# A decoder layer on one core: a rearranged input stage (meta tokens' statistics on ScalarE, first tiles loaded by halves on two queues, bias products moved ahead, first group's splits moved back)

## Chip, core and metric

The kernel runs on one NeuronCore of a Trainium2 chip. The metric is the device time of one execution in microseconds (us). Engines are called as in the profile: PE (TensorE, matrix products and transposes), PEld (its weight loads), DVE (VectorE), ACT (ScalarE), POOL (GpSimd) and SP (SyncE, which here only issues DMAs). DMAs are issued from SP's queue and from ACT's queue.

## The reference

One layer of a hybrid decoder over 1024 tokens of width 1024, with 16 meta tokens put in front. What touches the change is the beginning:

```
h = concatenate([meta_tokens, x])              # 16 + 1024 rows
h = layer_norm(h, in_ln_g, in_ln_b)            # over 1024 columns, eps 1e-5
z = h @ w_in + b_in                            # split into q | k | v | conformer input | gates
...
bias_of(d) = rel_bias[t5_bucket(d)]            # a table of 32 buckets x 8 heads, spread over distances
```

Behind it come sliding-window attention with sinks and the T5 bias, a gated causal convolution, the merge of both by two gates, a residual with a layer norm, and a convolutional feed-forward block with a second residual and norm.

## The kernel before

All activations stay transposed (channels on partitions, tokens on the free axis). Each float32 product is made of three products of rounded halves: an operand is split into `hi` (rounded, a cast on ACT or DVE) and `lo` (the rest, a subtraction on DVE), and PE forms hi·hi, hi·lo and lo·hi.

**The input stage** (lines 170 to 613) has to bring x and the meta tokens in, normalise them, transpose them on PE and make the first three column tiles of z: tile 0 is k, tile 1 is v, tile 2 is the first quarter of q. Tokens come in eight tiles x0 to x7 of 128 rows; the 16 meta rows are tile -1. They are held twice, on partitions 0 to 31 of `xm`, and the normalised ones are written to partitions 96 to 127. Work goes by three groups: group 0 is the meta rows with x0 and x1 (272 columns), group 1 x2 to x4, group 2 x5 to x7 (384 each).

For each group the steps are: `stat` (two bn_stats over 512 columns and one aggregate, on DVE), `table` (reciprocal root, ACT), `newton` (one Newton step in small DVE operations), `norm` (x·r + m in halves of 512 columns, on DVE or ACT), `turns` (PE transposes, 128 channels `k` at a time, into PSUM banks; there are four such banks, tags s and t), `scaled` (ACT: gain and bias of the layer norm, from PSUM to SBUF, which frees the bank), `parts` (the hi and lo of the result), and the products. Group 0 takes a short cut: its first products (`z_first(..., raw=True)`) are plain float32 products of the unsplit operands, so that no split is waited for; its `parts` are only needed by later tiles of z. The groups 1 and 2 go through `lagged`, in which the three tiles follow one another at two steps' distance.

`warm` are 28 products of a matrix of ones that PE does while nothing is there yet. `whi0` and `wlo0` split the first three weights. `evac` empties the sums: k into `kd`, v into `vT`, q (scaled, split) into `qd`.

**Order.** The tile framework orders each engine's instructions by a simulated timeline: lower ranks go first (`rank`, `tc.cur_priority`), and what is ready goes. For the input stage the order is written out by hand: `in_order` gives three chains, `dv`, `ac` and `pe`, whose instructions keep the order of the source on DVE, ACT and PE. What is issued outside these chains (evacuations, loads) finds its place by rank. `load` issues on SP's queue, `store` on ACT's. A queue issues in order, and a waiting entry holds the ones behind it.

**The bias table.** `tab` holds one-hot rows for 564 distances and the 33 x 8 table. Two products (400 and 164 columns) give `vrow`, which goes to DRAM (`v1d`), is spread over 128 partitions (`vd`) and read with skewed patterns into the attention's bias tiles. Before, these products stand on PE behind the third group's last product.

**After the stage** come `residual` (DVE makes h0 for the residual from the normalised tiles, and SP stores it to `h0d`) and `conv_chunk`, whose first two weights (`wt_c1`) are split early. `z_tile` makes one column tile of z over the token groups `ZG` (400, 384 and 256 columns) in the order of the list.

Of the kernel before, what the change touches and what calls it, by code (L numbers as in the profile page):

```python
# [101 lines left out]
def tile_hybrid_layer(  # L102
# [68 lines left out]
    with rank(0):  # L171
        nc.vector.memset(eps, EPS)
        nc.scalar.activation(small.tile([P, 1], F, name="sq"), eps, AF.Abs_reciprocal_sqrt)
# [31 lines left out]
    with rank(25):  # L205
        load(tab[:33], table_in)
# [14 lines left out]
    nc.vector.memset(ones, 1.0 / CW)  # L221
    qb = const.tile([P, 4], F, name="qb")
# [50 lines left out]
    def weights(shape, fill):  # L273
# [4 lines left out]
        with rank({1: 13, 2: 18, 3: 17, 4: 23}.get(n, RK_SPLIT)):  # L278
            last_fill.append(fill(raw))
# [63 lines left out]
    def q_evac(r):  # L343
        def evac(g, a, b, ps):
# [5 lines left out]
            for hl, (put, x) in enumerate(((store, f32(h)), (load, f32(l)))):  # L350
# [48 lines left out]
    def newton(t):  # L399
# [6 lines left out]
        dv(stt(m_, mv[:, :, 0], -1.0, r_, OP.mult, OP.mult))  # L406
# [7 lines left out]
    def norm(t, j, on_dve):  # L414
# [3 lines left out]
        if j < 0:  # L418
            xns[j], to = xm, xm[96:]
        else:  # L420
            xns[j] = to = sp.tile([P, D], F, name="xn", tag="xn", bufs=4) if j < 4 else OB[:, (j - 4) * D:(j - 3) * D]
        for a in range(0, D, 512):
            if on_dve:
                dv(V.tensor_scalar(to[:, a:a + 512], x_[:, a:a + 512], r_[:n, i:i + 1], m_[:n, i:i + 1], OP.mult, OP.add))
            else:
                ac(nc.scalar.activation(to[:, a:a + 512], x_[:, a:a + 512], AF.Identity, bias=m_[:n, i:i + 1],
# [117 lines left out]
    norm(1, 0, True)  # L544
    norm(1, 1, False)
    turns(0, 0, 1, 2, 3)
    stat(2, 2, 3, 4)
# [7 lines left out]
    z_first(0, (0,), 5, 6, 7, raw=True)  # L555
    table(2)
    newton(2)
    whi0(0)
# [3 lines left out]
    z_first(0, (2,), 0, 1, 2, 3, 4, raw=True)  # L562
# [4 lines left out]
    z_first(0, (2,), 5, 6, 7, raw=True)  # L567
# [31 lines left out]

    tc.cur_priority = RK_RESID + 1000  # L600
    vrow = sp.tile([NH, J_LEN], F, name="vrow")
    for a, b in ((0, 400), (400, J_LEN)):
        ps = pat.tile([P, 512], F, name="ps_v", tag="o" if a == 0 else "t", bufs=1 if a == 0 else 2)
        after(nc.tensor.matmul(ps[:NH, :b - a], tab[:, J_LEN:], tab[:, a:b], start=True, stop=True), pe_done[-1])
        after(nc.vector.tensor_copy(vrow[:, a:b], ps[:NH, :b - a]), first_nm)
    load(v1d, vrow)
# [4 lines left out]
    residual(3, -1, 0, 1, 2, 3)  # L611
# [1130 lines left out]
```

## Time and profile before

| | |
|---|---|
| runs (us) | 1282.33, 1282.07, 1282.24; median 1282.24 |
| the profiled execution | 1282.14 us, span 1280.0 us |
| PE, DVE, ACT, POOL busy | 99%, 84%, 46%, 4% of the span |
| granted PE clock, mean | 0.999 |
| DMA | 212.10 MB, 166 GB/s on average; near 420 GB/s from 9 to 19 us |

The page gives busy shares, the span in 40 slices, the DMA queues, the chain of work that ended last and the costliest groups of instructions. The answers of the trace used below are: the chain of waits in order of time (start, duration, what the end of the kernel waited for), tables of busy time in chosen stretches (PE, PEld, DVE, ACT, POOL, granted clock, DMA share, GB/s), groups of instructions by form (count, busy us, mean ns, idle time before and what ended it), the timeline, and the DMA view (packets, sizes, issues, median us from issue to landing). A line number is that of the code above; L117 and L113 are the helpers `store` and `load`.

### The profile page before, as it was taken

The page shows a single profiled execution, that of the slowest core. Times are in us where ns is not written, and L with a number is a line of the kernel's source. Part 1 is how long each engine was busy: PE and PEld are TensorE (multiplying, and loading weights), DVE is VectorE, ACT ScalarE, POOL GpSimd, SP SyncE. Part 2 cuts the span into 40 slices and gives each one's busy share as a digit, 9 for nine tenths or more (in the row PEclk, how much of TensorE's full clock was granted, in tenths as well). Part 3 has the DMA queues.
Part 4 walks back from the last instruction along what each step waited for, and adds up shares of the span by engine and source line. Part 5 has one row for each costly group of instructions (what it writes and reads, how often), then busy time and mean ns, then how long its engine had stood idle before and what let it go on. Part 6 is the DMA issues. An engine that isn't in the chain of part 4 may idle for free.

```text
span 1280.0 us, 21674 instructions
## 1 busy us (share of the span) xinstructions
PE 1267.9 (99%) x8546; PEld 1192.8 (93%) x8546; DVE 1078.7 (84%) x1830; ACT 585.5 (46%) x1063; POOL 53.8 (4%) x28
## 2 busy tenths in 40 slices
PE   9999999999999999999999999999999999999997
PEld 8999999999999999788999999999999997888886
DVE  7899989999987577548899898988989876987697
ACT  7523245545482233344655555455454453435330
POOL 0000000010112231000000000000000000000000
PEclk9999999999999999999999999999999999999999
DMA  7284633332247354222145545454454566989712
GB/s 274 73 306 108 180 95 100 98 95 88 75 136 232 111 157 116 83 99 77 56 172 190 191 178 198 163 194 149 157 190 171 192 242 238 392 291 349 269 60 83
DMA packets 96152, 212.10 MB, mean 166 GB/s; under 512 B 10787, under 2 KB 35939, under 8 KB 95922
## 3 DMA queue, kind: packets, MB, share of 16 engines
q1 hardware_dynamic: 84282, 199.64, 46.1%
q10 hardware_dynamic: 11768, 11.08, 2.7%
q8 instruction: 67, 1.10, 0.4%
q14 instruction: 35, 0.29, 0.1%
HBM read 150.29 MB, written 62.70 MB: 166 GB/s over the span
## 4 chain that ended last, share of the span: by engine, by line
PE 96%; DVE 2%; DMA 1%; ACT 0%; issue 0%; SPq 0%; DVEq 0%; ACTq 0%
PE px L1463 15%; PE py L1463 10%; PE ps_x L1588 9%; PE ps_z L298 8%; PE ps_z L294 8%; PE ps_z L299 8%; PE ps_z L1588 5%; PE pw L1463 5%; PE pz L1463 5%; PE ps_p L298 2%; PE ps_p L299 2%; PE ps_p L294 2%; PE ps_w L294 2%; PE ps_w L299 2%; PE ps_w L298 2%; PE ps_z L510 2%
## 5 line engine op out<-in xcount | busy, mean ns | idle before, releaser
L662 DVE SCALAR_TENSOR_TENSOR FA<-cin,cols,FA 128x1026 f32<-128x1026 f32 x120 | 155.2, 1305 | 0.2
L294 PE MATMUL ps_z<-RHO,whi 128*128 128x384 f32 (+2 forms) x324 | 105.0, 324 | 0.0
L298 PE MATMUL ps_z<-RHC,whi 128*128 128x384 f32 (+2 forms) x324 | 104.9, 324 | 0.0
L299 PE MATMUL ps_z<-RHC,wlo 128*128 128x384 f32 (+2 forms) x324 | 104.2, 321 | 0.0
L298 PE MATMUL ps_z<-RHO,whi 128*128 128x384 f32 (+2 forms) x324 | 104.1, 321 | 0.0
L294 PE MATMUL ps_z<-RHC,whi 128*128 128x384 f32 (+2 forms) x324 | 103.9, 321 | 0.0
L299 PE MATMUL ps_z<-RHO,wlo 128*128 128x384 f32 (+2 forms) x324 | 103.3, 319 | 0.0
L1285 DVE TENSOR_TENSOR RHO<-wr,RHO 128x512 fp32r<-128x512 f32 x94 | 63.5, 684 | 10.3 <-ACT RHO L1284 10.3
L1284 ACT CAST RHO<-wr 128x512 fp32r<-128x512 f32 x94 | 56.8, 620 | 21.3 <-DVE wr L1302 10.5
L265 ACT CAST whi<-wr 128x1024 fp32r<-128x1024 f32 x37 | 38.9, 1052 | 59.4 <-PE ps_z L298 42.0
L294 PEld LDWEIGHTS ps_z<-RHO,whi 128*128 128x128 f32 x324 | 60.9, 188 | 0.6 <-issue 0.3
L299 PEld LDWEIGHTS ps_z<-RHC,wlo 128*128 128x128 f32 x324 | 61.1, 188 | 0.4
L298 PEld LDWEIGHTS ps_z<-RHC,whi 128*128 128x128 f32 x324 | 60.9, 188 | 0.4
L294 PEld LDWEIGHTS ps_z<-RHC,whi 128*128 128x128 f32 x324 | 60.8, 188 | 0.3
L298 PEld LDWEIGHTS ps_z<-RHO,whi 128*128 128x128 f32 x324 | 60.9, 188 | 0.2
L299 PEld LDWEIGHTS ps_z<-RHO,wlo 128*128 128x128 f32 x324 | 61.0, 188 | 0.1
L1302 DVE TENSOR_TENSOR wr<-wr 128x512 f32<-128x512 f32 x88 | 60.1, 683 | 0.2
L1475 ACT COPY FA<-px 128x514 f32<-128x514 f32 (+2 forms) x23 | 13.1, 571 | 81.6 <-PE px L1463 81.6
L268 POOL TENSOR_TENSOR wlo<-wr,whi 128x1024 fp32r<-128x1024 f32 x17 | 42.0, 2474 | 188.4 <-ACT whi L265 177.1
L669 ACT ACTIVATE FA<-ps_z,cols 128x386 f32<-128x386 f32 (+2 forms) x48 | 26.0, 541 | 51.3 <-PE ps_z L299 46.9
L1285 DVE TENSOR_TENSOR ws<-wr,ws 128x512 fp32r<-128x512 f32 x60 | 40.6, 685 | 6.1 <-ACT ws L1284 6.0
L1463 PE MATMUL px<-OA,RHO 128*128 128x258 f32 x324 | 43.5, 283 | 0.0
(456 smaller groups left out, 3583.5 us busy)
## 6 DMA issues: line engine op xcount, KB each, us to landing
wr<-in_w_up_dram SPq DMA_DIRECT2D x44, 512.0 KB, 4.2
wr<-in_w_z_dram SPq DMA_DIRECT2D x30, 512.0 KB, 6.2
fd<-FA SPq DMA_DIRECT2D x44, 256.0 KB, 2.4
OB<-in_w_down_dram SPq DMA_DIRECT2D x21, 512.0 KB, 4.8
FA<-sd SPq DMA_DIRECT2D x15, 512.0 KB, 8.0
qt<-qd SPq DMA_DIRECT2D x28, 256.0 KB, 3.9
td<-OB SPq DMA_DIRECT2D x12, 512.0 KB, 3.2
sums<-fd SPq DMA_DIRECT2D x12, 512.0 KB
```

Of the source, the lines that this page charges most:

```text
L265: ins = nc.scalar.copy(hi, raw)
L268: return (nc.vector if quick else nc.gpsimd).tensor_tensor(lo, raw, f32(hi), OP.subtract)
L294: ins = nc.tensor.matmul(ps, ah, bh, start=i == 0, stop=False)
L298: nc.tensor.matmul(ps, ah, bl, start=False, stop=False)
L299: last = nc.tensor.matmul(ps, al, bh, start=False, stop=i == n - 1)
L662: nc.vector.scalar_tensor_tensor(acc[c], cin[:, j:j + U], wc, acc[c], OP.mult, OP.add)
L669: nc.scalar.activation(t, ps, AF.Tanh, bias=bcol(14 + i), scale=0.5)
L1284: nc.scalar.copy(hi, src)
L1285: ins = nc.vector.tensor_tensor(lo, src, f32(hi), OP.subtract)
L1302: ins = nc.vector.tensor_tensor(*x)
L1463: ins = nc.tensor.matmul(o, x[:, ks], bmat(sub, q, hl, k), start=first and k + j == 0, stop=k == 3 and j == 2, skip_group_check=not first)
L1588: nc.tensor.matmul(banks[i], l[:, ts], r[:, ws], start=first and a and x + k == 0, stop=z and x == len(ops) - 1 and k == 2, skip_group_che ...
```

## The change

- The 16 meta rows are loaded twice by one DMA with a source that repeats them (stride 0), not by two DMAs.
- x0 is loaded in two halves of 512 columns on ACT's queue, ahead of ACT's first instruction; x1 in two halves on SP's. The ranks of the other loads change: the bias table now before the first weight, the third weight before x3.
- The meta tokens' mean, variance, reciprocal root and Newton step go from DVE to ACT (`meta_norm`): two passes over 1024 columns with accumulators, six one-column operations. Group 0's Newton step on DVE then has three operations, not four; `norm` on DVE takes (x - mean)·r and no longer needs m.
- The first normalisations go in three pieces (256, 256, 512 columns); x1's are now on DVE too. The first transposes are of two values of k, then of two more, not of four at once.
- The warm-up has 21 products, not 28. The two products with the bias table follow it; DVE copies their result between the statistics of x2 and x3, and `v1d` is stored there.
- Tile 2 makes all eight raw products of group 0 before the second group's transposes (before: five before, three behind).
- The split of tile 1's weight moves behind the fourth scaling of group 1; statistics of x6 and x7 move back by one or two channels.
- The third group's transposes and products are interleaved in smaller pieces; the splits of group 0 (`parts(0, ...)`) move behind the whole third group, their `hi` onto ACT.
- The first group's stores of k and of the first q part go on SP's queue.
- The first conv chunk's gate tile takes its token groups in the order 1, 2, 0; `residual` begins with x1.

```diff
     with rank(0):
         nc.vector.memset(eps, EPS)
+        x0 = sp.tile([P, D], F, name="x0", tag="x", bufs=8)
+        for a in range(0, D, 512):
+            store(x0[:, a:a + 512], x[0, :P, a:a + 512])
         nc.scalar.activation(small.tile([P, 1], F, name="sq"), eps, AF.Abs_reciprocal_sqrt)
...
     with rank(5):
-        for i in range(2):
-            load(xm[i * NMETA:(i + 1) * NMETA], meta_tokens)
-    xt = []
+        load(xm[:2 * NMETA], dram(meta_tokens, 0, [[0, 2], [D, NMETA], [1, D]]))
+    xt = [x0]
...
-        load(t, x[0, j * P:(j + 1) * P, :])
+        for a, b in ((0, 512), (512, D)) if j == 1 else ((0, D),):
+            load(t[:, a:b], x[0, j * P:(j + 1) * P, a:b])
         xt.append(t)
 
-    for j in range(NB):
-        with rank((10, 11, 14, 15, 16, 20, 21, 22)[j]):
+    for j in range(1, NB):
+        with rank((0, 10, 20, 24, 26, 30, 32, 34)[j]):
             load_x(j)
...
-    with rank(12):
+    with rank(14):
         load(cols, cols_in)
...
-    with rank(25):
+    with rank(16):
         load(tab[:33], table_in)
...
+    c15, eps_h = (const.tile([P, 1], F, name=n) for n in ("c15", "eps_h"))
+    nc.vector.memset(c15, 1.5)
+    nc.vector.memset(eps_h, -0.5 * EPS)
...
-        with rank({1: 13, 2: 18, 3: 17, 4: 23}.get(n, RK_SPLIT)):
+        with rank({1: 18, 2: 28, 3: 22, 4: 36}.get(n, RK_SPLIT)):
...
-    def z_tile(fill, groups, evac, wt=None):
+    def z_tile(fill, groups, evac, wt=None, order=(0, 1, 2)):
         wt = wt or weights([P, KC, P], fill)
-        for g, (a, b) in enumerate(groups):
-            z_group(wt, g, a, b, evac)
+        for g in order:
+            z_group(wt, g, *groups[g], evac)
...
-        store(kd[:, a:b], t)
+        (load if g == 0 else store)(kd[:, a:b], t)
...
-            for hl, (put, x) in enumerate(((store, f32(h)), (load, f32(l)))):
+            for hl, (put, x) in enumerate(((load if g == 0 and r == 0 else store, f32(h)), (load, f32(l)))):
...
-        dv(stt(m_, mv[:, :, 0], -1.0, r_, OP.mult, OP.mult))
+        if t > 1:
+            dv(stt(m_, mv[:, :, 0], -1.0, r_, OP.mult, OP.mult))
...
+    def meta_norm():
+
+        n = 2 * NMETA
+        norms[0] = [None] + [sp.tile([P, 1], F, name=f"{n_}0") for n_ in "trm"]
+        nm, var, v_ = (sp.tile([P, 1], F, name=n_)[:n] for n_ in ("nm", "varm", "vm"))
+        _, t_, r_, m_ = (x_ if x_ is None else x_[:n] for x_ in norms[0])
+        junk = OB[:n, 3 * D:4 * D]
+        act = lambda *a, **k: ac(nc.scalar.activation(*a, **k))
+        act(junk, xm[:n], AF.Identity, scale=-1.0 / D, accum_out=nm)
+        act(junk, xm[:n], AF.Square, bias=nm, scale=1.0, accum_out=var)
+        act(v_, var, AF.Identity, bias=eps_h[:n], scale=-0.5 / D)
+        act(r_, var, AF.Abs_reciprocal_sqrt, bias=eps[:n], scale=1.0 / D)
+
+        act(t_, r_, AF.Identity, scale=v_)
+        act(t_, t_, AF.Identity, bias=c15[:n], scale=r_)
+        act(r_, t_, AF.Identity, scale=r_)
+        act(m_, nm, AF.Identity, scale=r_)
...
-        for a in range(0, D, 512):
+        for a, b in zip(cuts, cuts[1:]):
             if on_dve:
-                dv(V.tensor_scalar(to[:, a:a + 512], x_[:, a:a + 512], r_[:n, i:i + 1], m_[:n, i:i + 1], OP.mult, OP.add))
+                dv(V.tensor_scalar(to[:, a:b], x_[:, a:b], mv[:n, i, 0:1], r_[:n, i:i + 1], OP.subtract, OP.mult))
...
-                with rank(24):
+                with rank(38):
                     load(gb[i], dram(ln0_in, i * D, [[0, P], [1, D]]))
...
-    warm = pat.tile([P, 512], F, name="ps_w", tag="o")
-    for i in range(28):
+    warm = pat.tile([P, 512], F, name="ps_w", tag="mm", bufs=3)
+    for i in range(21):
         pe(nc.tensor.matmul(warm[:, :P], ones, ones, start=True, stop=True))
-    stat(0, -1)
-    table(0)
+    vrow = sp.tile([NH, J_LEN], F, name="vrow")
+    vps = []
+    for a, b in ((0, 400), (400, J_LEN)):
+        ps = pat.tile([P, 512], F, name="ps_v", tag="mm" if a else "o", bufs=3 if a else 1)
+        pe(nc.tensor.matmul(ps[:NH, :b - a], tab[:, J_LEN:], tab[:, a:b], start=True, stop=True))
+        vps.append((a, b, ps))
     stat(1, 0)
-    newton(0)
-    norm(0, -1, False)
+    meta_norm()
     stat(1, 1)
     table(1)
+    cuts = (0, 256, 512, D)
+    for c in zip(cuts, cuts[1:]):
+        norm(0, -1, False, c)
+    newton(1)
+    for c in zip(cuts, cuts[1:]):
+        norm(1, 0, True, c)
+        norm(1, 1, True, c)
+    turns(0, 0, 1)
+    turns(0, 2, 3)
+    stat(2, 2)
+    for a, b, ps in vps:
+        dv(V.tensor_copy(vrow[:, a:b], ps[:NH, :b - a]))
+    with rank(40):
+        load(v1d, vrow)
+    stat(2, 3)
     scalings()
-    newton(1)
-    norm(1, 0, True)
-    norm(1, 1, False)
-    turns(0, 0, 1, 2, 3)
-    stat(2, 2, 3, 4)
+    stat(2, 4)
...
+    whi0(0)
     table(2)
     newton(2)
-    whi0(0)
...
-    z_first(0, (2,), 0, 1, 2, 3, 4, raw=True)
+    z_first(0, (2,), *range(8), raw=True)
     evac(0, 0)
     wlo0(0)
     whi0(2)
     turns(1, 0, 1, 2, 3)
-    z_first(0, (2,), 5, 6, 7, raw=True)
     z_first(0, (1,), *range(8), raw=True)
...
     for k in range(8):
         scaled(1, k)
+        if k == 3:
+            whi0(1)
         parts(1, k, hi_act=(k,))
-        if k == 1:
-            whi0(1)
+        if k == 3:
             wlo0(1)
-        if k in (3, 6):
-            stat(3, 6 if k == 3 else 7)
+        if k in (5, 7):
+            stat(3, 6 if k == 5 else 7)
...
-    lagged(1, (0, 2, 1), range(8))
+    lagged(1, (0, 2, 1), range(9))
     turns(2, 0, 1, 2, 3)
-    lagged(1, (0, 2, 1), range(8, 10))
-    turns(2, 4, 5, 6, 7)
-    lagged(1, (0, 2, 1), range(10, 12))
+    lagged(1, (0, 2, 1), range(9, 12))
     for k in range(8):
         scaled(2, k)
         parts(2, k, hi_act=(1, 3, 5, 7))
-        if k in (3, 4, 5, 6):
-            parts(0, 2 * k - 6, 2 * k - 5)
-    lagged(2, (0, 2, 1), range(12))
+        if k == 1:
+            turns(2, 4, 5)
+            lagged(2, (0, 2, 1), range(2))
+        elif k > 1:
+            if k == 3:
+                turns(2, 6, 7)
+            lagged(2, (0, 2, 1), (k,))
+    lagged(2, (0, 2, 1), range(8, 12))
+    parts(0, *range(8), hi_act=range(8))
     first_nm = dv_done[-1]
-
-    tc.cur_priority = RK_RESID + 1000
-    vrow = sp.tile([NH, J_LEN], F, name="vrow")
-    for a, b in ((0, 400), (400, J_LEN)):
...
-    load(v1d, vrow)
...
-    residual(3, -1, 0, 1, 2, 3)
+    residual(3, 1, -1, 0, 2, 3)
...
-        z_tile(in_cols(10 + c), ZG, g_evac, wt_c1[0] if c == 1 else None)
+        z_tile(in_cols(10 + c), ZG, g_evac, *((wt_c1[0], (1, 2, 0)) if c == 1 else ()))
```

More of the change, by code (lines that the diff above doesn't have):

```diff
@@ L412, in scalings, with norm @@
         dv(V.tensor_scalar(nsink, sink, -1.0, None, OP.mult))
-    def norm(t, j, on_dve):
+    def meta_norm():
[13 more added lines that the diff above has]
+        act(m_, nm, AF.Identity, scale=r_)
+    def norm(t, j, on_dve, cuts=(0, 512, D)):
         x_, n = src_of(j)
@@ L419, in norm @@
             xns[j], to = xm, xm[96:]
+        elif j in xns:
+            to = xns[j]
         else:
             xns[j] = to = sp.tile([P, D], F, name="xn", tag="xn", bufs=4) if j < 4 else OB[:, (j - 4) * D:(j - 3) * D]
-        for a in range(0, D, 512):
+        for a, b in zip(cuts, cuts[1:]):
             if on_dve:
-                dv(V.tensor_scalar(to[:, a:a + 512], x_[:, a:a + 512], r_[:n, i:i + 1], m_[:n, i:i + 1], OP.mult, OP.add))
+                dv(V.tensor_scalar(to[:, a:b], x_[:, a:b], mv[:n, i, 0:1], r_[:n, i:i + 1], OP.subtract, OP.mult))
             else:
-                ac(nc.scalar.activation(to[:, a:a + 512], x_[:, a:a + 512], AF.Identity, bias=m_[:n, i:i + 1],
+                ac(nc.scalar.activation(to[:, a:b], x_[:, a:b], AF.Identity, bias=m_[:n, i:i + 1],
                                         scale=r_[:n, i:i + 1]))
@@ L594, in tile_hybrid_layer @@
         parts(2, k, hi_act=(1, 3, 5, 7))
-        if k in (3, 4, 5, 6):
-            parts(0, 2 * k - 6, 2 * k - 5)
-    lagged(2, (0, 2, 1), range(12))
-    first_nm = dv_done[-1]
-    tc.cur_priority = RK_RESID + 1000
-    vrow = sp.tile([NH, J_LEN], F, name="vrow")
-    for a, b in ((0, 400), (400, J_LEN)):
-        ps = pat.tile([P, 512], F, name="ps_v", tag="o" if a == 0 else "t", bufs=1 if a == 0 else 2)
-        after(nc.tensor.matmul(ps[:NH, :b - a], tab[:, J_LEN:], tab[:, a:b], start=True, stop=True), pe_done[-1])
-        after(nc.vector.tensor_copy(vrow[:, a:b], ps[:NH, :b - a]), first_nm)
-    load(v1d, vrow)
+        if k == 1:
[7 more added lines that the diff above has]
+    parts(0, *range(8), hi_act=range(8))
+    first_nm = dv_done[-1]
     tc.cur_priority = RK_QKV + 3000
```

## The prediction

> **What bounds the kernel now.** First the page: engine totals, and the shares of the chain that ended last.
>
> ```profile
> span 1280.0 us, 21674 instructions
> PE 1267.9 (99%) x8546; PEld 1192.8 (93%) x8546; DVE 1078.7 (84%) x1830; ACT 585.5 (46%) x1063; POOL 53.8 (4%) x28
> ...
> PE 96%; DVE 2%; DMA 1%; ACT 0%; issue 0%; SPq 0%; DVEq 0%; ACTq 0%
> ```
>
> PE is the bound nearly everywhere, so the change can win only where PE does not yet do work that counts, or where it does work that could lie elsewhere. The chain of waits over the first 70 us (start, us, what) shows where:
>
> ```profile
> 0.74 0.40 SPq L113
> ...
> 1.65 3.97 DMA x<-in_x_dram
> ...
> 5.64 1.30 DVE st L391 x2
> ...
> 7.78 1.46 ACT xm L426 x2
> ...
> 9.32 0.30 ACT r L397
> ...
> 9.64 0.17 DVE t L403
> ...
> 9.84 0.17 DVE t L404
> ...
> 10.43 0.56 DVE xn L424
> ...
> 11.03 1.11 PE ps_h L460 x8
> ...
> 12.16 0.58 ACT FA L466
> ...
> 12.79 0.73 PE ps_z L507 x2
> ...
> 16.21 4.01 PE ps_z L507 x18
> 20.22 1.31 PE ps_h L460 x12
> 21.53 4.97 PE ps_z L507 x22
> ...
> 56.06 1.05 PE ps_v L604 x4
> ```
>
> Until 12.79 the chain runs over the load of x0, statistics, a Newton step (9.64 to 10.43), the first normalised half, nine transposes and one scaling. From 12.79 on it is PE alone: I call this moment P0. A table of busy time by stretches (length, PE busy, instructions, clock, DMA share, GB/s) confirms it and dates the warm-up:
>
> ```profile
> 1.00:7.20 6.20, 6.12 (x28) 1.00 0.79 256
> 7.20:10.30 3.10, 3.10 (x30) 1.00 1.01 407
> ...
> 12.80:56.10 43.30, 43.30 (x253) 1.00 0.39 138
> ```
>
> So the whole question is: how much earlier is P0, what leaves the PE stream behind it, and does the stream stay unbroken. All sums are made against the profiled execution, 1282.14 us (1280.0 of span and 2.1 around it); the median of the runs, 1282.24, lies 0.10 above it.
>
> **Bias products, minus 1.05.** The two products with the table (56.06, 1.05 us) move behind the warm-up. Their cover is idle PE: the warm-up is cut from 56 instructions to 42. The first 28 take until 7.2, the other 14 go at 3.10/28 = 0.11 us, to about 8.75; the bias products then end at 9.8. The first useful transpose must be later than that, or the 1.05 is partly paid again. They also wait for the table's load, and every transpose stands behind them on PE; that load is now ahead of the first weight, behind x1 and the columns on SP, and by the reckoning below (151 KB on the slowest engine, 5.8 us at 26 GB/s, from the 2 us at which the first data move) it is there near 8, before the warm-up ends.
>
> **The meta tokens' load.** Two loads of 16 rows become one, whose source is [2 copies, 16 rows, 1024]. The trace has one store of that form: line 809 writes 16 rows as [2 blocks, 8 heads, 128]. The DMA view in the stretch that holds the first meta load alone, then in the one that holds that store:
>
> ```profile
> DMA packets 35, 0.08 MB, mean 35 GB/s; under 512 B 16, under 2 KB 16, under 8 KB 35
> ```
>
> ```profile
> DMA packets 18, 0.01 MB, mean 4 GB/s; under 512 B 2, under 2 KB 18, under 8 KB 18
> ...
> rd<-rt ACTq DMA_DIRECT2D x1, 8.0 KB
> ```
>
> The meta load of 16 rows has 16 tiny packets beside its data; the store of 16 pieces has two. I read a tiny packet as the end of one DMA engine's share, so the store ran on two engines, as many as its outermost dimension counts. The new meta load has two there. Prices, from the DMA view and the table of stretches:
>
> ```profile
> xm<-in_meta_tokens_dram SPq DMA_DIRECT2D x2, 64.0 KB, 2.2
> ```
>
> ```profile
> 9.00:11.00 2.00, 1.61 (x15) 1.37 (x13) 1.58 (x10) 1.16 (x3) 0.00 (x0) 1.00 1.03 420
> ```
>
> 420 GB/s is 26 GB/s an engine, 0.157 us for a row of 4 KB. Issued at 0.74, with 2.2 us for one row an engine, the 32 rows land at 3.1 if 16 engines share them, at 0.74 + 2.2 + 15 x 0.157 = 5.3 if two do, and at 6.5 if these two carry their 32 KB of x0 (1.25 us) in between. I take 5.7: two engines, and not all of x0 ahead.
>
> [...]
>
> **The meta statistics on ACT.** Rows by form (count, busy us, mean ns):
>
> ```profile
> L466 ACT ACTIVATE tm<-ps_h,cols 128x384 f32<-128x384 f32 x16 | 10.3, 675 | 2.1 <-PE ps_h L460 2.0
> ...
> L484 ACT CAST whi<-wr 128x1024 fp32r<-128x1024 f32 x3 | 3.1, 1041 | 0.0
> ...
> L474 ACT CAST RHO<-tm 128x384 fp32r<-128x384 f32 x6 | 3.1, 512 | 0.1
> ...
> L426 ACT ACTIVATE xm<-xm,m,r 32x512 f32<-32x512 f32 x2 | 1.5, 802 | 2.5 <-DVE m L406 2.5
> ...
> L346 ACT ACTIVATE FA<-ps_z,qb 128x258 f32<-128x258 f32 x1 | 0.5, 465 | 0.0
> L348 ACT CAST qsh<-FA 128x258 fp32r<-128x258 f32 x1 | 0.4, 408 | 0.0
> ...
> L397 ACT ACTIVATE r<-mv,eps 32x1 f32<-32x1 f32 x1 | 0.3, 293 | 2.8 <-DVE mv L392 2.8
> ```
>
> ```profile
> L842 ACT ACTIVATION_READ_ACCUMULATOR s<-s,sm 128x1 f32 x64 | 12.0, 187 | 0.0
> ```
>
> Two passes over 1024 columns cost 2.1 (twice 1.04) to 2.4 (from two times 0.80 less overlap, plus a pointer); I take 2.2. Each has an accumulator read, 0.19, together 0.35. Six one-column operations at 0.29, nearly all dependent, 1.75. That is 4.3 us after the landing; then the table for x0 and x1 (0.30) and three Newton steps at 0.195 (9.64 to 9.84), 0.6. So group 0's factors, T, stand 5.2 us after the landing: 10.9, where before they stood at 10.43. DVE no longer sets this: x1's second half waits on the two loaded engines for 64 + 32 + 32 KB (4.9 us), lands near 7.2, and its statistics end near 8.0, two us before ACT needs them. The two x0 issues on ACT push its table load back, which has until 5.7.
>
> **From T to P0.** Before: 12.79 - 10.43 = 2.36. After: a quarter-width pass on DVE (half of 0.56, and 0.04), five transposes instead of nine before the scaling, the others under it. But ACT must first do three pieces of the meta rows (0.5, 0.5, 0.8 from 0.6 before T), so scaling starts near T + 1.1, ends at T + 1.7: P0 is T + 1.73, or 12.65. Gain 0.15; with the landing at 5.3 it is 0.55, with 6.5 it is a loss of 0.65.
>
> **The stream behind P0.** Three products of tile 2 (4.01/9 = 0.45 each) move ahead of the second group's transposes: same work. They give DVE and ACT time, and both need it. DVE after T: six pieces of x0 and x1 2.2, three statistics at 1.42 (two halves at 0.674 and the aggregate) and more, the scalings 0.25, and the copies of the bias products, which it had at 63 us (first the statistics, by form, then the copies):
>
> ```profile
> L391 DVE BATCH_NORM_STATS2 st<-x 128x6 f32<-128x512 f32 x16 | 10.1, 674 | 0.7 <-DMA x<-in_x_dram 0.7
> ```
>
> ```profile
> L605 DVE COPY vrow<-ps_v x2: 306/430/555, 62.9 to 63.3; 8x400 f32<-8x400 f32 x1, 8x164 f32<-8x164 f32 x1
> ```
>
> That is T + 7.5, P0 + 5.8; table, four Newton steps and ACT's two passes bring P0 + 8.4. PE reaches the transposes at P0 + 3.42 + 12 x 0.45 = P0 + 8.8, and they begin on the first half: 1.1 us of cover. Its second four transposes, at P0 + 13.7 (as 20.22 + 1.31 + 4.97 - 12.79 before), need banks that ACT's first four scalings free; the fourth is needed at P0 + 14.4. ACT has from P0 + 8.4: a split 1.04, the q evacuation 0.47 + 0.41, four scalings and three casts at 1.12 a pair, 4.04: P0 + 14.4. Between 0 and 0.8 of stall (if the k evacuation falls in it too); I take 0.3. The kd and first q stores leave ACT for SP, which spares ACT three issues here; the split of tile 1 moves behind the fourth scaling, which is what makes this fit.
>
> The last product of the third group shows what the first group's splits cost in their old place (PE's timeline, a pair that elsewhere takes 0.51):
>
> ```profile
> 50.92 0.78 PE L510 MATMUL ps_z<-RHC,whi 128*128 128x384 f32 x2
> ```
>
> With them behind it, 0.27 is won. They are needed by the first chunk's tile, whose order becomes 1, 2, 0, some 7 us later: hidden. The queue's new order (the third weight before x3, table before the first weight) is behind P0's needs.
>
> **Sum.** -1.05 - 0.15 + 0.3 - 0.27 = -1.15: 1281.0. Of this 1281.0 the landing's ends make 1280.6 and 1281.8, the ACT stall 1280.7 and 1281.5.
>
> **Rivals.** *The meta load runs on all 16 engines.* For it: 16 rows a copy. Against: the store above. Landing 3.1, T = 8.3; now PE binds: warm-up and bias products hold it until 9.8, then 12 transposes at 0.11, P0 = 11.1, 1.7 earlier. With 1.05 and 0.27: 1279.1, with the ACT stall 1279.4; I say 1279.2. Anything else that shortens the chain ends there too.
>
> *The second group comes late.* The two loaded engines hold back every later tile by the extra 64 KB, 2.3 us, and x4 now also lies behind a weight (1.25). SP's waits show that its queue already stops for landings:
>
> ```profile
> SPq L113 <- DMA x<-in_x_dram: 3.1, 4, 0.9
> ```
>
> ```profile
> x<-in_x_dram SPq DMA_DIRECT2D x8, 512.0 KB, 7.2
> ```
>
> ```profile
> 3.53 1.71 SPq L113 DMA_DIRECT2D x<-in_x_dram  x3
> ```
>
> x4, the last of the three issued from 3.53 to 5.24 before, landed near 12; then near 16. DVE wants it at P0 + 4.3 = 17.0, so 1 us is cover. If SP's stops grow by as much as they are now (3.1), x4 lands at 19, and 2.1 us go through statistics, norm and transposes to PE one for one, with the ACT stall at 0.8 behind them: 1281.0 + 2.1 + 0.5 = 1283.6, slower than before; from a landing later than 18.3 it decides the sign. With the meta rows at 6.5, 1284.4, and a reordered tail of the stage can add some tenths to a whole microsecond.
>
> **Chances.** 0.2% is 2.56 us, about what a measurement of this kernel can tell from no change. Forecast 0.50 (its own range 1280.0 to 1282.3), all 16 engines or an equal shortening 0.28, late second group 0.22. Faster by over 0.2% means below 1279.7: three quarters of the second case and a tenth of the first, 0.26. Slower means above 1284.8: the third case with a long stop or a reordered stage, 0.6 of it, and a little of the first, 0.15. The rest, 0.59, is within. The range runs from 1278.8 (the second case without a stall and a little more) to 1284.6 (the third case).
>
> **What would show it.** The new meta load: 2 tiny packets beside 32 rows, landing at 5.3 to 6.5 and not 3.1. The chain of waits before P0: meta load, two ACT passes, small ACT operations, table, Newton, instead of x0 and DVE. Bias products near 8.8 to 9.8 with PE idle behind them. P0 near 12.65; transposes of the second group at P0 + 8.8 without a wait; a short wait for a scaling at P0 + 14; no long pair at the end of the third group; the first chunk about 1.15 earlier than 57.1. I am wrong if P0 is before 11.5, if PE waits over 1 us between P0 and the first chunk, or if the 1215 us behind it change length.

## The result, and the profile after

| | before | changed |
|---|---|---|
| runs (us) | median 1282.55 (1281.90 to 1283.13, 10 runs) | median 1286.17 (1283.77 to 1287.41, 10 runs) |
| ratio | | 1.0027, 95% interval 1.0018 to 1.0037 |
| profiled execution | 1282.14, span 1280.0 | 1287.41, span 1285.0 |
| granted PE clock, mean | 0.999 | 0.996 |

The changed kernel is 3.6 us slower than before, and 1286.17 lies outside the predicted range. Its profiled execution is the slowest of its ten: 5.27 above that of before.

The chain of waits of the changed kernel (start, duration, what the end waited for) shows the input stage:

```profile
2.96 7.45 DMA tab<-in_table_dram
...
10.54 1.11 PE ps_v L566 x4
11.65 1.82 issue
13.47 2.97 PE ps_h L487 x12
...
60.35 0.18 PE ps_z L300
```

The first chunk begins at 60.35; before it was 57.10. The first 12 transposes take 2.97 us, though before 8 of them took 1.11. PE waited until 10.54 for the bias table, then 1.82 us for the normalised tokens. The timeline of the same kernel (start, duration, what ran, and in brackets how long the engine had been idle and what ended that) tells why they were late:

```profile
0.74 0.80 SPq L113 DMA_DIRECT2D xm<-in_meta_tokens_dram  x1
...
1.08 6.95 PE L561 MATMUL ps_w<-ones 128*128 128x128 f32 x42 [1.08 <-DVE half L230]
...
3.78 0.76 SPq L113 DMA_DIRECT2D x<-in_x_dram  x1
8.22 0.33 SPq L113 DMA_DIRECT2D wr<-in_w_z_dram  x1
8.23 1.06 ACT L428 ACTIVATE OB<-xm 32x1024 f32<-32x1024 f32 x1 [5.08 <-DMA xm<-in_meta_tokens_dram]
8.48 0.69 DVE L397 BATCH_NORM_STATS2 st<-x 128x6 f32<-128x512 f32 x1 [4.31 <-DMA x<-in_x_dram]
...
12.47 0.28 ACT L403 ACTIVATE r<-mv,eps 128x2 f32<-128x2 f32 x1
...
13.37 2.30 DVE L451 TENSOR_SCALAR xn<-x,mv,r 128x256 f32<-128x256 f32 x6
...
16.23 0.66 PE L534 MATMUL ps_z<-FA,wr 128*128 128x272 f32 x1
```

The meta rows, issued at 0.74, let ACT start at 8.23 only. x0's second half came to DVE at 8.48, the table to PE at 10.54: what goes through the same two DMA engines is late as well. By the semaphores of this trace the last two increments for the rows came at 7.46 and 8.21; of the 16 for x0's second half 14 came by 5.48 and two at 7.73 and 8.46, of the table's 12 ten by 8.87 and two at 10.06 and 10.40. SP issued nothing between 4.54 and 8.22; it waited 3.7 us for the rows' landing. The factors stand at 13.37, 5.14 after the landing, and P0 is 16.23 instead of 12.79.

The trace's first record of the granted clock is at 5.29; the clock falls to a half at 12.12 and rises at 18.95, 6.83 us later. A table of stretches of half that length, 3.41 us, from 5.29 on (length, PE busy and instructions, clock, DMA share, GB/s) shows the second loss:

```profile
5.29:8.71 3.42, 2.74 (x25) 1.00 0.99 309
8.71:12.12 3.41, 1.11 (x4) 1.00 0.99 384
12.12:15.53 3.41, 2.06 (x9) 0.50 1.02 401
15.53:18.95 3.42, 3.42 (x14) 0.50 1.03 419
18.95:22.36 3.41, 3.41 (x21) 1.00 0.92 338
```

After a stretch in which PE was busy for 1.11 of 3.41 us, its clock falls to a half and stays there until 18.95. The first transposes and z products run in this time: two z products take 0.91 us at 17.99 and 0.46 at 19.31 (chain of waits). From P0 to the first chunk PE has no wait, yet needs 44.1 us without the bias products, where before it took 44.3 with them.

Behind the first chunk the offset to before grows from 3.25 to 5.0 at the end of the span; the other 0.27 of the 5.27 lies outside the span. Most of the growth within the span is in the up-projection. Its 400 us from 640 on, and one of its groups (count, busy us, mean ns), before:

```profile
640.00:1040.00 400.00, 400.00 (x3370) 400.00 (x3369) 363.56 (x581) 209.34 (x347) 0.00 (x0) 1.00 0.51 182
```

```profile
L1463 PE MATMUL px<-OC,ws 128*128 128x256 f32 x204 | 26.7, 280 | 0.0
```

and in the changed kernel:

```profile
640.00:1040.00 400.00, 400.00 (x3357) 400.00 (x3357) 362.03 (x580) 208.57 (x346) 0.00 (x0) 1.00 0.50 177
```

```profile
L1500 PE MATMUL px<-OC,ws 128*128 128x256 f32 x204 | 26.9, 281 | 0.0
```

PE is busy all the time at full clock in both, but in the changed one it does 13 products fewer, at 400/3370 = 0.119 us each 1.5 us. No line of the diff lies in this stage. Time less span is 2.1 us (2.06 to 2.18) in all runs of before and of the kernels made from it, 2.2 to 2.7 in all runs of the changed kernel and of those made from it. What it consists of isn't shown.

### The profile page after: what moved, and what is told of

It is laid out like the page before. It is cut to its first block, busy times and chain, and to the rows that moved or that the text cites. A ratio compares the mean times of both kernels' runs of the same rounds, so it can differ in the third digit from the quotient of the medians.

```text
span 1285.0 us, 21649 instructions
## 1 busy us (share of the span) xinstructions
PE 1268.7 (99%) x8532; PEld 1194.2 (93%) x8532; DVE 1074.3 (84%) x1820; ACT 591.2 (46%) x1079; POOL 55.3 (4%) x28
## 4 chain that ended last, share of the span: by engine, by line
PE 94%; DMA 2%; DVE 2%; issue 0%; ACT 0%; POOL 0%; DVEq 0%; SPq 0%; POOLq 0%
PE px L1500 14%; PE py L1500 9%; PE ps_x L1625 9%; PE ps_z L304 8%; PE ps_z L300 8%; PE ps_z L305 8%; PE ps_z L1625 5%; PE pz L1500 5%; PE pw L1500 5%; PE ps_p L304 2%; PE ps_p L305 2%; PE ps_p L300 2%; PE ps_w L300 2%; PE ps_w L304 2%; PE ps_w L305 2%; PE ps_z L537 2%
## 5 line engine op out<-in xcount | busy, mean ns | idle before, releaser
L300 PE MATMUL ps_z<-RHO,whi 128*128 128x384 f32 (+3 forms) x324 | 104.9, 324 | 0.0
L304 PE MATMUL ps_z<-RHC,whi 128*128 128x384 f32 (+3 forms) x324 | 104.8, 324 | 0.0
L305 PE MATMUL ps_z<-RHC,wlo 128*128 128x384 f32 (+3 forms) x324 | 104.1, 321 | 0.0
L304 PE MATMUL ps_z<-RHO,whi 128*128 128x384 f32 (+3 forms) x324 | 104.0, 321 | 0.0
L300 PE MATMUL ps_z<-RHC,whi 128*128 128x384 f32 (+3 forms) x324 | 103.8, 320 | 0.0
L305 PE MATMUL ps_z<-RHO,wlo 128*128 128x384 f32 (+3 forms) x324 | 103.2, 319 | 0.0
```

Of the source, the lines that this page charges most:

```text
L300: ins = nc.tensor.matmul(ps, ah, bh, start=i == 0, stop=False)
L304: nc.tensor.matmul(ps, ah, bl, start=False, stop=False)
L305: last = nc.tensor.matmul(ps, al, bh, start=False, stop=i == n - 1)
```

## The experiments

The theories: that the one load of the meta rows runs on two DMA engines and delays all that needs these (A); that the gaps on PE let the clock fall, whatever makes them (B); and that a part is lost in the up-projection (C), by where the tiles now lie (L) or by the order that the new stage leaves behind (O). Each run went with runs of before on the same chip; the table gives medians against these.

| kernel | us | against before |
|---|---|---|
| changed | 1286.17 | +3.62, ratio 1.0027 [1.0018, 1.0037] |
| two meta loads | 1281.68 | -0.58, 0.9996 [0.9987, 1.0005] |
| one load, long warm-up | 1284.00 | +1.74, 1.0014 [1.0005, 1.0023] |
| before, with the one load | 1288.17 | +5.91, 1.0044 [1.0030, 1.0058] |
| two loads, bias products in their old place | 1286.34 | +4.08, 1.0029 [1.0019, 1.0039] |
| two loads, no shift | 1280.45 | -1.64, 0.9986 [0.9977, 0.9995] |
| before, shifted by 64 bytes | 1283.42 | +1.33, 1.0011 [1.0003, 1.0020] |
| before, shifted by 128 bytes | 1283.88 | +1.79, 1.0012 [1.0003, 1.0021] |
| no shift, x0 on SP's queue | 1280.45 | -1.64, 0.9988 [0.9979, 0.9997] |
| the same, meta rows and table first | 1280.62 | -1.60, 0.9987 [0.9978, 0.9996] |
| changed, [2, 16] other rows | 1286.03 | one run |
| changed, [4, 8] other rows | 1283.99 | one run |

### The load alone, taken back

```diff
-        load(xm[:2 * NMETA], dram(meta_tokens, 0, [[0, 2], [D, NMETA], [1, D]]))
+        for i in range(2):
+            load(xm[i * NMETA:(i + 1) * NMETA], meta_tokens)
```

> The changed kernel, with the meta rows loaded by two DMAs of 16 rows each, as before the change. Theory A (the loss is the one load, whose 32 rows run on two DMA engines and hold up all that follows on these two): the rows land near 3 us instead of 8.2, the factors of group 0 stand near 8.5 instead of 13.4 (landing + 5.2), x0's second half, the columns and the table land up to 2 us earlier; PE then is held by its own warm-up and the bias products until 9 to 9.8, the first z product begins at 11.1 to 11.8 instead of 16.2, no gap of more than 1 us on PE, no half clock behind 7 us: 1279 to 1280.5 us. Theory B (the loss is the granted clock, which falls in PE's gaps, whatever the load does): the gaps stay, since warm-up is shorter and the bias products wait for the table; a stretch at half clock before 19 us remains and the time is 1282 to 1285. Theory C (part of the loss, 1.7 us, arises in the up stage from the new layout of buffers): the first chunk is 3 to 4 us earlier but the time is only down to 1281.5 to 1283, with the 1215 us behind it still longer than before.

Measured: 1281.68. The chain of waits:

```profile
1.19 3.64 DMA xm<-in_meta_tokens_dram
...
9.25 0.20 ACT r L404
10.06 0.42 DVE xn L452
10.53 1.42 PE ps_h L488 x11
11.95 0.69 PE ps_z L535 x2
...
54.80 0.18 PE ps_z L301
```

The rows land at 4.83, not near 3: x0's halves now come at the same time from the other queue. Factors stand at 10.06 (landing + 5.23), P0 is 11.95, the first chunk 54.80, 5.55 earlier than in the changed kernel; there is no stretch at half clock. A holds for the start, with a landing that I had put too early; the time missed A's forecast (1279 to 1280.5) and fell into C's. But the first chunk is 2.30 earlier than before the change, and the profiled execution (1281.72) only 0.42 shorter: 1.9 us go again behind it. Of these 0.5 lie outside the span (it is 1279.1 long, before 1280.0). The other 1.4 are C, with 3357 products in the up-projection's 400 us as in the changed kernel. L and O below divide C.

### The clock alone

```diff
-    for i in range(21):
+    for i in range(36):
         pe(nc.tensor.matmul(warm[:, :P], ones, ones, start=True, stop=True))
```

> The changed kernel with its one load of the meta rows, but with 36 warm-up products in place of 21, so that PE is busy until 11 to 12 us. It prices the granted clock alone. Theory B: no half clock between 12 and 19 us, factors of group 0 still at 13.4, but the first z product at 15.0 to 15.3 instead of 16.2 (bias products then end near 12 to 13, before the transposes) and 0.8 less behind it: 2 us less than the changed kernel, 1283.5 to 1284.5. If the clock costs nothing that the end sees, the time stays at 1286, or rises a little by the longer warm-up.

Measured: 1284.00, 2.2 below the changed kernel and within the forecast. The load still takes until 7.36 (chain of waits, first row), and PE, which the additional products keep busy, stays at full clock (a stretch):

```profile
0.74 6.62 DMA xm<-in_meta_tokens_dram
...
14.41 0.69 PE ps_z L534 x2
```

```profile
8.76:12.17 3.41, 3.41 (x28) 2.73 (x26) 2.46 (x7) 3.22 (x10) 0.00 (x0) 1.00 1.03 396
```

So of what the load costs (4.2 us, from +3.62 to -0.58) up to 1.9 go through the clock: useless work on PE made the kernel faster. A part of this comparison is that the rows landed earlier here. In the two profiled executions the first chunks are 3.09 us apart (57.26 here): 0.85 by the landing, and 2.2 by the clock, 0.97 between the factors and P0 and 1.27 behind P0. But that execution of the changed kernel is the slowest of its ten.

### The one load put into the kernel before

```diff
-        for i in range(2):
-            load(xm[i * NMETA:(i + 1) * NMETA], meta_tokens)
+        load(xm[:2 * NMETA], dram(meta_tokens, 0, [[0, 2], [D, NMETA], [1, D]]))
```

> The kernel before, with only the load of the meta rows replaced by the one DMA with the repeated source. It prices the load alone. Theory A: the rows land between 5.3 and 8.5 us on two DMA engines instead of near 3, the meta statistics stand first in DVE's order, so the first z product moves from 12.8 to 14.5 to 16.5, perhaps with a stretch at half clock behind it: 1284.5 to 1288. If the load is harmless by itself (the loss sits in the statistics on ScalarE, or in the halves of x0 and x1 on two queues): 1282 to 1283, as before.

Measured: 1288.17, 0.2 above the upper end; P0 came at 17.06, later than the forecast 16.5. Nothing of the rest of the change is in it. Its load landed at 7.64, its clock fell after a stretch with 0.30 us of PE work; one with 2.82 did not raise it, and only at the end of a full one, at 20.68, it was whole again:

```profile
0.74 6.90 DMA xm<-in_meta_tokens_dram
```

```profile
10.44:13.86 3.42, 0.30 (x1) 0.14 (x1) 2.85 (x16) 1.85 (x4) 0.00 (x0) 1.00 1.03 422
13.86:17.27 3.41, 2.82 (x12) 2.42 (x13) 3.38 (x7) 2.32 (x4) 0.00 (x0) 0.50 1.02 419
17.27:20.68 3.41, 3.41 (x11) 2.71 (x12) 1.70 (x5) 1.84 (x5) 0.00 (x0) 0.50 1.03 407
20.68:24.10 3.42, 3.42 (x19) 2.84 (x18) 0.89 (x5) 2.86 (x6) 0.00 (x0) 1.00 0.26 103
```

x0 is issued behind the rows on the same queue here, so the landing can be this late without pieces of x0 ahead of the rows. By the packet records of this trace the rows began at 2.31, and the first row on each of the two engines took 1.07 us.

### The bias products back in their old place

```diff
-    for i in range(21):
+    for i in range(26):
         pe(nc.tensor.matmul(warm[:, :P], ones, ones, start=True, stop=True))
...
+    tc.cur_priority = RK_RESID + 1000
+    vrow = sp.tile([NH, J_LEN], F, name="vrow")
+    for a, b in ((0, 400), (400, J_LEN)):
...
+    load(v1d, vrow)
```

(on top of the two meta loads)

> As the changed kernel with two meta loads, but the two bias products, their copies and the store stand behind the third group's last product again, as before the change, and the warm-up has 26 products in place of 21, so that PE is busy about as long. It measures what the move of the bias products is worth. If they lie under idle PE in the changed kernel: 1.05 us slower than the changed kernel with two loads (1280.2 to 1281.5 against 1279 to 1280.5). If they cost at their new place what they cost at the old one (the table comes late, transposes queue behind them): equal to it within 0.4 us, with an earlier first z product.

Measured: 1286.34, 4.7 slower than with two loads alone; a miss by over 3 us. In its profiled execution (1285.03) the chain has the products where they were put, and the first chunk 1.13 later than the 54.80 above:

```profile
12.02 0.70 PE ps_z L535 x2
...
54.88 1.05 PE ps_v L640 x4
55.93 0.37 PE ps_z L301
```

P0 is the same but for 0.07, so 1.06 is what the move is worth at this place, as the prediction had it. The other 2.2 by which this execution exceeds that with two loads (1285.03 against 1281.72) lie far behind, the largest of them in two waits of PE that the kernel with two loads doesn't have:

```profile
PE px L1499 <- DVE OB L1254: 0.9, 1, 0.9
PE ps_z L1624 <- DVE RHC L1587: 0.8, 1, 0.8
```

They end at 614 and 1083 us, at the seams of stages. Around the first, DVE's and ACT's instructions stand in the same order in both kernels, so why PE waits in one of them stays open. Another 1.3 lie between this execution and the median. A part of them may be the clock: of the nine runs, the four at 1286.3 to 1286.5 have a mean granted clock of 0.996 or 0.997, the four at 1284.9 to 1285.7 of 0.998 or 0.999; the slowest, 1287.1 with 0.998, does not fit.

### The constants out of the lasting pool

```diff
-    c15, eps_h = (const.tile([P, 1], F, name=n) for n in ("c15", "eps_h"))
+    c15, eps_h = (sp.tile([P, 1], F, name=n) for n in ("c15", "eps_h"))
```

(on top of the two meta loads)

> The changed kernel with two meta loads, and with the two new constants of ScalarE (c15, eps_h) allocated in the input stage's own pool instead of among the lasting constants, so that weights, operands and results of all later stages lie 64 bytes a partition lower, as before the change; no instruction is added, removed or reordered. Theory L (the slow growth in the up-projection, 13 products fewer in the 400 us from 640 to 1040, comes from where the tiles lie): 3368 to 3371 products in this stretch, 1.5 us less than the kernel with two loads: 1279.8 to 1280.5. Theory O (it comes from the order or the timing that the new input stage leaves behind): 3356 to 3360 products there, 1281.4 to 1282.

Measured: 1280.45, 1.23 less than with two loads alone, at the edge of what L expected, with as many instructions on every engine:

```profile
640.00:1040.00 400.00, 400.00 (x3370) 400.00 (x3369) 362.86 (x580) 208.31 (x344) 0.00 (x0) 1.00 0.51 182
```

3370 products, as before the change. L holds, O falls. The other kernels agree: all that have the two constants in the lasting pool do 3356 to 3358 products in this stretch, all others 3369 or 3370, whatever their start.

### The same 64 bytes put into the kernel before, and 128

```diff
-    nc.vector.memset(ones, 1.0 / CW)
+    nc.vector.memset(ones, 1.0 / CW); [nc.vector.memset(const.tile([P, 1], F, name=n), 1.5) for n in ("c15", "eps_h")]
```

> The kernel before with nothing but the two constants added among the lasting constants (two memsets of 0.06 us on DVE, never read), which moves every later tile of the left side by 64 bytes a partition. Theory L: 3356 to 3360 products in the 400 us from 640 to 1040 instead of 3370, 1.5 us slower, 1283.5 to 1284. Theory O: 3369 to 3371 there, 1282.2 as before.

Measured: 1283.42 (+1.33), just under the 1283.5 that L expected, with 3358 products. And with four constants in place of two:

> The kernel before with four such constants, so that the later tiles of the left side move by 128 bytes. If theory L holds and what counts is the place of a tile within 128 bytes: as before the change, 1282.2 with 3368 to 3371 products from 640 to 1040. If any shift costs (distances between tiles, or the sum of the sizes): 1283.5 or more. Theory O: 1282.2 as well, so that this kernel tells something only if the one with 64 bytes is slower.

Measured: 1283.88 (+1.79). The stretch in the first and in the second of these:

```profile
640.00:1040.00 400.00, 400.00 (x3358) 400.00 (x3357) 361.72 (x578) 207.92 (x345) 0.00 (x0) 1.00 0.50 180
```

```profile
640.00:1040.00 400.00, 400.00 (x3356) 400.00 (x3356) 361.56 (x578) 207.54 (x344) 0.00 (x0) 1.00 0.50 180
```

Two constants that nobody reads make the kernel 1.3 us slower, in a stage that begins 600 us after they are written. Weights, operands and results on the left side (wr, whi, RHC, RHO, OA) lie further by what the constants take, by my reckoning of the framework's allocation 64 bytes a partition (an estimate: the traces hold no addresses); OC, allocated from the other end, stays. That the old speed comes back after 128 bytes is ruled out. What in the chip makes a product some 0.5 ns longer is not shown.

### x0 on SP's queue, and the order of the loads

```diff
-        for a in range(0, D, 512):
-            store(x0[:, a:a + 512], x[0, :P, a:a + 512])
+        with rank(6):
+            for a in range(0, D, 512):
+                load(x0[:, a:a + 512], x[0, :P, a:a + 512])
```

(on top of two loads and no shift)

> The changed kernel with two meta loads and without the shift, and with x0's two halves issued on SP's queue behind the meta loads instead of on ScalarE's queue at the same time. If the meta rows are late because x0's pieces share the DMA engines with them (second load landed at 4.83 with x0 beside it, 3.36 before): they land near 3.4, the ACT chain (landing + 5.2) ends near 8.6 to 8.9, and the first z product begins at 10.4 to 10.8 instead of 11.95, with x1's statistics ready by 8.2: 1278.6 to 1279.3, and 1 to 1.4 us faster than the kernel that differs in this alone. If x0 and x1 come so much later that DVE's statistics set the end: equal to it within 0.4 us.

Measured: 1280.45, equal. The planner put x0's first half between the two meta loads, so these landed at 4.71 again; and now the table was last to come:

```profile
4.00 4.99 DMA tab<-in_table_dram
9.12 1.11 PE ps_v L568 x4
...
11.82 0.69 PE ps_z L536 x2
```

Then the meta rows before x0 (rank 8) and the table before the columns (rank 12):

> As the kernel with x0 on SP's queue, but with the ranks set so that both meta loads are issued first (there x0's first half stood between them, and the second meta load landed at 4.71) and the bias table before the columns (it landed near 9.0, and the bias products waited 0.5 us for it). If the start is set by the meta rows' landing and the table's: the meta rows land near 3.4, ScalarE's chain and x1's statistics end near 8.4, group 0's factors stand at 9.1 instead of 9.9, the bias products end by 9.5, the first z product begins at 10.9 to 11.2 instead of 11.8: 1279.4 to 1279.9, 0.6 to 1 us less. If x1 comes later by what was put ahead of it, or the columns by the table, the gain is gone: 1280.2 to 1280.7.

Measured: 1280.62, equal again. The meta rows land at 3.46 and their statistics are done 1.2 us earlier, but now x1's second half lands at 8.07:

```profile
3.06 5.01 DMA x<-in_x_dram
8.09 0.70 DVE st L399
...
9.98 0.42 DVE xn L453
...
11.87 0.69 PE ps_z L536 x2
```

In these three kernels (no shift, and the two with x0 on SP's queue) another chain ends last each time: the meta rows on ACT, the table on PE, x1 on DVE. P0 is 12.10, 11.82 and 11.87, within 0.3 us. Whether x0 goes on two queues or one makes no difference to the time. All three are faster than both given kernels, than the one before by 1.6 us.

### Two blocks or two copies, and four blocks

```diff
-        load(xm[:2 * NMETA], dram(meta_tokens, 0, [[0, 2], [D, NMETA], [1, D]]))
+        load(xm[:2 * NMETA], dram(x, 0, [[512 * D, 2], [D, NMETA], [1, D]]))
```

> The changed kernel, with the one load of 32 rows reading [2 blocks, 16 rows, 1024] of x in place of [2 copies, 16 rows, 1024] of the meta tokens: rows 0 to 15 and 512 to 527 of x stand where the meta tokens belong, so the two copies are no longer the same rows and the layer is that of other tokens. If the late landing (8.2) comes from the outermost dimension of 2, which puts the load on two DMA engines: 2 tiny packets, landing again between 7.4 and 8.3, 1284 to 1287 us. If it comes from reading the same rows twice (stride 0): landing near 4.8 as with two loads, 1281.5.

Rows of x stand where the meta tokens belong, so this kernel leaves the meta tokens out and only its times count. And with `[[256 * D, 4], [D, 8], [1, D]]`:

> The same with [4 blocks, 8 rows, 1024] of x, the same 32 rows of 4 KB by one DMA, but with an outermost dimension of 4 (again other tokens' rows in place of the meta tokens). Four engines with 8 rows each instead of two with 16: 4 tiny packets, and by 0.3 us for a row (the two-engine load took 6.9 us from issue to landing, 2.2 of it for the first row) a landing 2.5 us earlier, 5.2 to 6, group 0's factors at 10.4 to 11.2, 1282 to 1283.5 us. If the number of engines doesn't follow the outermost dimension: as the kernel with two blocks.

Measured: 1286.03 and 1283.99. The chain's first step of the two:

```profile
0.74 7.18 DMA xm<-in_x_dram
```

```profile
0.74 4.80 DMA xm<-in_x_dram
```

Two blocks land at 7.92, four at 5.54, within the forecast 5.2 to 6. Different rows are as late as the same rows twice, so the repeated source is innocent, and in these two runs the outermost dimension decided: the load's semaphore got two late increments with two blocks (7.85, 7.92) and four with four (4.68 to 5.54); the rest came at once, by 2.0. With four blocks the time missed its forecast (1282 to 1283.5), and the clock fell here too.

Eight rows fewer on an engine landed 2.38 us earlier, 0.30 for each row of 4 KB, the price that the forecast had used. But that is not what a row takes, and the forecast came true by luck. The packet records of the two traces give 0.159 us for most rows (the median in both), as the prediction had it. With four blocks all rows lay between 2.74 and 4.62, and the last increment came 0.9 later. With two blocks pieces of x0 from ACT's queue (2 KB, 0.084 us and more) went between the later rows, which began 0.24 to 0.36 apart. In the kernel with the long warm-up, whose load of two blocks landed at 7.36, the same difference is 1.82, or 0.23 for a row.

## Why the prediction was wrong

**The landing: the step that failed.** The step on the meta tokens' load read rightly that it would run on two engines; the changed kernel (two late increments, at 7.46 and 8.21) and the runs with two blocks (two) and four (four) show it. The price of the landing was wrong: 5.7 was taken from a range of 5.3 to 6.5, and it was 8.2 in the profiled execution, 7.4 to 7.9 in those with two blocks or a longer warm-up. The upper bound was therefore none.

The term for a row was right (0.157 us; the median in the packet records is 0.159). The choice between the ends was not: of x0, "not all" was to be ahead, but the records show the rows beginning at 2.97, where the first data of before moved at 1.77, with a half of x0 ahead of them and pieces of the other half in between. And the sum had no term for packets that take several times their usual time. Strung together by their times, the packets of one of the two engines are: eight pieces of x0 from 1.78 to 2.96, the first 0.59 long and not 0.08; sixteen rows, the second 0.64 long and not 0.16, the later ones alternating with x0, until about 6.7; landing 7.46. The two long packets make 1.0 us more, about what this engine exceeds 6.5 by. The other engine's share landed 0.75 later still, at 8.21; why it did stays open. The table was reckoned with all that the two engines carry, and yet came at 10.4 instead of near 8, and x1's second half at 9.5 instead of 7.2: the same missing time.

**The ACT chain was right.** 5.2 us from the landing to the factors were forecast; 5.14 and 5.23 were measured. So of the 3.58 us by which P0 missed 12.65, 2.5 are the landing, and 1.1 lie between the factors and P0 (2.86, not 1.73).

**The clock was missing.** Without it the late landing moves P0 by the landing's own delay. With it the transposes and products until 18.95 ran at a granted clock of 0.50, up to 1.9 us more in the medians. The view that I used to date the warm-up has the clock in each row, but the sum had no term for what a shorter warm-up and a PE that waits twice would do to it. The sign did not hang on it alone: with the long warm-up the kernel is still 1.7 slower than before.

**The rival on the slower side was not the one that came.** Between P0 and the first chunk PE waited 0.1 us at most in the runs with the new order: the second group was not late. SP did stop for landings, as that rival had it, from 4.54 to 8.22 in the changed kernel, but nothing behind P0 waited for what it held back.

**The other steps.** The bias products' move was worth 1.06 (1.05 forecast), once the table comes in time. The stall of 0.3 did not appear, and the long pair at the end of the third group is gone; the stream from P0 to the first chunk took 42.85 with two loads, where before it took 44.31 - 1.05 = 43.26: 0.41 less, where the sum had 0.03 more. From the factors to P0 it was 1.89 at full clock, not 1.73.

**The part that nobody would look for.** "If the 1215 us behind it change length" was on the list of what would prove me wrong, and they did. Two constants of 4 bytes a partition move the tiles of the left side and cost 1.3 us in the up-projection. In the diff this was one line, in the prediction two memsets.

Together, against before: the load +4.2 (up to 1.9 of it by the clock), the shift +1.1, all the rest of the change -1.64. That this is near the forecast of -1.15 is partly luck. In the profiled execution without load and shift P0 comes 0.69 earlier (the sum had 0.15), the bias products' move wins 1.05, the stream takes 0.51 less (the sum had 0.03 more), and 0.86 is lost again behind the first chunk, 0.51 of it outside the span, where the sum had nothing.

## What to carry to other kernels

Before two DMAs become one, look at the outermost dimension of the access pattern, and add up for the few engines all that they carry, from either queue. Here 32 rows landed at 4.83 from two DMAs, at 5.54 from one of four blocks and at 7.36 to 8.21 from one of two; even that sum came out 0.9 to 1.7 us too early, and the table (10.40) and x1's second half (9.47) were late as well. In a short prologue ask, for each 3.4 us, how much work PE keeps: here a gap was paid once as a wait (1.82 us) and once more as half clock (6.83 us long), and the kernel with 15 more warm-up products, which do nothing, was 2.2 us faster. When a late stage changes its speed without any change in its code, count its instructions in a fixed stretch, and move new small constants out of the pool in front of the big tiles; here that was worth 1.23 us.

## What was not expected of the hardware

- **The clock fell behind stretches in which PE was busy for a part of the time.** In the input stage half clock lasted 3.41 us (four blocks, two blocks of other rows) or 6.83 (changed kernel; before, one load). In stretches of 3.41 us from the first clock record of each trace, which lay anywhere from 4.13 to 7.19 us in the profiled executions, those with 1.11 (changed kernel) and 0.30 (before, one load) of work were followed by half clock. With four blocks it was 1.42, with two blocks of other rows 1.58:

```profile
7.77:11.18 3.41, 1.42 (x6) 0.44 (x6) 2.13 (x8) 3.22 (x12) 0.00 (x0) 1.00 1.03 411
11.18:14.59 3.41, 3.41 (x14) 3.07 (x15) 3.38 (x9) 2.75 (x6) 0.00 (x0) 0.50 1.02 411
```

```profile
10.31:13.72 3.41, 1.58 (x7) 0.61 (x8) 1.26 (x6) 3.22 (x11) 0.00 (x0) 1.00 1.02 402
13.72:17.13 3.41, 3.41 (x15) 3.07 (x15) 3.38 (x9) 2.65 (x5) 0.00 (x0) 0.50 1.03 420
```

  In the kernel with the meta rows and the table first, 1.93 were enough to keep it:

```profile
7.54:10.96 3.42, 1.93 (x10) 0.94 (x11) 2.37 (x9) 2.18 (x6) 0.00 (x0) 1.00 1.00 389
10.96:14.37 3.41, 3.41 (x25) 2.81 (x24) 3.38 (x10) 3.25 (x7) 0.00 (x0) 1.00 1.03 419
```

  So in these runs 1.58 of 3.41 us (46%) were too little to keep it and 1.93 (56%) were enough. To rise again it took a full stretch: 2.06 (changed kernel) and 2.82 (before, one load) did not do, 3.41 did. How much an execution loses may depend on where its gaps fall on these stretches. The ten runs of the changed kernel, 1283.8 to 1287.4 with a mean clock of 0.998 to 0.995, fit this, but one by one it is not shown.
- **The load on few engines was late, though its rows were not slow.** It landed at 7.36 to 8.21 with two blocks and at 5.54 with four. Most rows took 0.159 us on two engines and on four, as in the price from 16 full ones (0.157). The time went into other packets on the same engines and into single packets of 0.6 to 1.07 us, for which no run here shows a reason.
- **Two constants more in front of the tiles** change 3370 products in 400 us to 3357, and with four (3356) the old speed did not come back.
